# Queries, keys and maxima as float16 pairs in an encoder's attention

## The chip, the cores and the metric

The kernel runs on one core of one Trainium2 chip. The metric is the device time of one execution in microseconds (us); before the change it is 2811.22 us, the median of 3 runs (2808.62 to 2813.11). The engines are PE (TensorE: the matmuls, with PEld for its weight loads), DVE (VectorE), ACT (ScalarE), POOL (GpSimd) and SP (SyncE, which issues the DMAs here).

## The reference

Two layers on a sequence of 2048 tokens with 1024 features, all in float32. Each layer norms its input, projects it, runs a gated mixer on one half of the features and attention on the other half, projects back and adds:

```
h    = rmsnorm(x, pre_g);  proj = h @ w_in
u_a, v_a, g_a, q, k, v, g_b = split(proj)      # 512,512,512,512,128,128,512 columns
y_a  = gmlp(u_a, v_a) * silu(g_a)
q    = rope(rmsnorm(q per head, q_norm_g));  k = rope(rmsnorm(k per head, k_norm_g))
p    = softmax(q k^T / 8)                       # 8 query heads, 2 key heads, 64 wide
y_b  = (p @ v) * silu(g_b)
x    = x + rmsnorm(concat(y_a, y_b) @ w_out, post_g)
```

The inputs `q_norm_g` and `k_norm_g` are about 8, so the scores are large and the products need more than one pass of a narrow type.

## The kernel before, in words

Most large products are taken in three passes over two parts: a tensor is split into a high part of type float32r (shown as f32 in the trace; below "float32r" means this type) and a low part, and high x high, high x low and low x high are added up in PSUM.

**Projection stage of a layer** (class `Project`). Tokens go in groups of 512. `hT_jobs` norms and transposes x, `do_kv` and `do_q` norm and rotate keys and queries (`norm_rope`), and later blocks make the mixer and the gates. In `do_kv` each 128-token tile of keys `kr` is split into a rounded copy, a second copy of it and a low part (tile `kk`: two ACT copies, one POOL subtraction); four transposes per tile (two of 128 columns, two of 64) bring them under each other, and copies put them into `k_st` (the high part twice, on 128 partitions) and `k_lo` (the low part on 64 partitions, and a row of ones on partition 64, written by one DMA per layer). `do_q` writes high and low queries to the DRAM tensor `q_d`.

**Attention stage** (`attend`). A unit is 512 queries of one head; there are 32 units in a layer, each of 16 steps, one step for 128 keys. Step `k` issues on PE two matmuls into the PSUM tile `sp` (`q_st` against `k_st`: both query parts against the high keys; `q2` against `k_lo`: the high queries against the low keys, and the row of ones against the row that holds minus the maximum and a shift). ACT takes the exponential twice (`p_hi` in float16, `p_f` in float32), POOL (85% of the steps) or DVE subtracts to get the low part `p_lo` in float16, and three steps later PE multiplies `p_hi` with the values (`po`, 128x128 stationary). Once per 8 steps a **burst** of 32 matmuls, each on 32 columns of the array, adds the low parts and the sums of the denominators (`po` and `sums`). Between these stand the `max_step`s of a later unit (`pmax`: one matmul, `q_m` stationary, `k_st` moving, then a DVE reduction; 16 per unit), and `fill`, the output projection's matmuls (`pout`). When a unit's maxima are there, `max_row` reduces them, `stack_max` transposes them on PE (`t`), ACT adds the shift and writes `m_rows`, and a DMA stores them in `m_d`, from where `load_q` fetches them as the last row of `q2`. The first 8 units of a layer (`PRE`) have their maxima taken in the projection stage.

**Order.** Inside the attention loop every PE, ACT, DVE and POOL instruction keeps the order in which the code issues it (`Pinned`). In the projection stage only the matmuls and some others are pinned; a scheduler places the rest, and SP's DMAs. Jobs given to `bg.add` run a set number of ticks later. PSUM tiles share a ring of 7 banks (`ps_t`). All `Pinned` calls have line 84 in the profile.

Of the kernel before, what the change touches and what calls it, by code (L numbers as in the profile page):

```python
# [9 lines left out]
F32 = mybir.dt.float32  # L10
F32R = mybir.dt.float32r
# [27 lines left out]
def encoder(ctx: ExitStack, tc, x, w_in, w_out, pre_g, post_g, ln_a_g, ln_a_b,  # L39
# [10 lines left out]
    big = ctx.enter_context(tc.tile_pool(name="big", bufs=7))  # L50
# [8 lines left out]
    def big_t(shape, name):  # L59
        return big.tile(shape, F32R, name=name, tag="big")  # L60
# [42 lines left out]
    q_d = [dram.tile([NH, 2, HD, GRP], F32, name=f"q_d{g}") for g in range(NG)]  # L103
    m_d = [dram.tile([NH, GRP], F32, name=f"m_d{g}") for g in range(NG)]
# [70 lines left out]
    class Project:  # L175
# [11 lines left out]
        def gains(self):  # L187
# [10 lines left out]
            nc.vector.tensor_scalar_mul(self.gain_q, self.gain_q, HD ** -0.5)  # L198
# [161 lines left out]
        def do_kv(self, g, banks):  # L360
# [6 lines left out]
            for i, kr in enumerate(krs):  # L367
                for j in range(2):
                    t = g * TPG + 2 * i + j
                    kk = f_t("kk", 3 * NKV * HD).rearrange("p (k a d) -> p k a d", k=NKV, a=3)  # L370
# [4 lines left out]
                    def trans(t=t, kk=kk):  # L375
# [4 lines left out]
                        nc.scalar.copy(k_st[:, :, t * P:(t + 1) * P],  # L380
                                       pk[:, 0:2 * P].rearrange("p (k s) -> p k s", k=NKV))
                        nc.vector.tensor_copy(k_lo[0:HD, :, t * P:(t + 1) * P],
                                              pk[0:HD, 2 * P:4 * P].rearrange("p (k s) -> p k s", k=NKV))
                    bg.add(KK_DELAY + 2 * (2 * i + j), trans)

        def do_q(self, g, banks, b):
            qrs = self.norm_rope([ps.rearrange("p (t h d) -> p t h d", t=2, d=HD) for ps in banks], 4,
                                 self.rope_rows(g, self.gain_q))
            for i, qr in enumerate(qrs):
                def trans(i=i, qr=qr):  # L390
# [4 lines left out]
                    hi = f_t("fh", dt=F32R).rearrange("p (k t) -> p k t", k=2)  # L395
                    lo = f_t("fl", dt=F32R).rearrange("p (k t) -> p k t", k=2)
                    nc.scalar.copy(hi, ps)
                    nc.vector.tensor_tensor(lo, ps, hi.bitcast(F32), ALU.subtract)
                    for a, part in enumerate((hi, lo)):
                        for h in range(2):  # L400
                            dst = q_d[g][4 * b + h:4 * b + 4:2, a, :, i * 2 * P:(i + 1) * 2 * P]
                            nc.sync.dma_start(dst.rearrange("k d t -> d k t"),
                                              part.bitcast(F32)[h * HD:(h + 1) * HD])
# [212 lines left out]
    def attend(l, kv, nxt):  # L616
# [31 lines left out]
        def load_qm(u):  # L648
            qb, h = units[u]
            s = state[u]  # L650
            s.qm = f_t("q_m", dt=F32R)
            nc.sync.dma_start(s.qm.bitcast(F32), q_d[qb][h].rearrange("a d t -> (a d) t"))
            s.mx = small.tile([P, TPG, NG], F32, name="mx", bufs=3)

        def load_q(u):
            qb, h = units[u]
            s = state[u]
            s.qs = f_t("q_st", dt=F32R)
            nc.sync.dma_start(s.qs.bitcast(F32), q_d[qb][h].rearrange("a d t -> (a d) t"))
            s.q2 = f_t("q2", dt=F32R)  # L660
            nc.sync.dma_start(s.q2.bitcast(F32)[0:HD], q_d[qb][h, 0])
            nc.sync.dma_start(s.q2.bitcast(F32)[HD:HD + 1], m_d[qb][h:h + 1])
# [14 lines left out]
        def stack_max(u, pe, act):  # L677
# [4 lines left out]
            rows = small.tile([TPG, P], F32R, name="m_rows")  # L682
            act.activation(rows, ps[0:TPG, 0:P], AF.Copy, bias=EXP_SHIFT)
            nc.sync.dma_start(m_d[qb][h].rearrange("(t p) -> t p", p=P), rows.bitcast(F32))
# [528 lines left out]
```

## Time and profile before

| what | value |
|---|---|
| median of 3 runs | 2811.22 us (2808.62 to 2813.11) |
| profiled execution | 2813.78 us |
| its span, first to last instruction | 2812.0 us |
| mean granted TensorE clock | 0.993 |
| busy: PE, PEld, DVE, ACT, POOL | 97%, 74%, 67%, 56%, 46% of the span |
| DMA queue | 290.57 MB, 33.1% of 16 engines |

Layer 0 projects from 0 to about 627 us and attends until about 1410 us; layer 1 follows the same pattern to the end. In the profile a matmul's row gives its start and a modelled duration; matmuls overlap in the pipeline, so the time that a matmul takes of PE is read from start to start of rows of a steady stream, not from its own duration. A matmul that is queued early (such as the `sp` after a `po`) shows an early start; there a whole step, from one second `sp` matmul to the next, is the sound measure.

### The profile page before, as it was taken

How to read it: one execution, taken by the hardware profiler on the slowest of the kernel's cores; microseconds unless marked ns; L12 is line 12 of the kernel's file. 1: busy time of each engine (PE TensorE's matmuls, PEld its weight loads, DVE VectorE, ACT ScalarE, POOL GpSimd, SP SyncE). 2: the span in 40 equal slices, each digit the busy share in tenths (PEclk: the TensorE clock that was granted, in tenths of full speed). 3: DMA queues.
4: the chain of work that ended last, by engine and by line, in shares of the span. 5: the costliest groups of instructions: out<-in, count | busy, mean ns of one | idle time of the engine just before them, and what ended most of it. 6: DMA issues, size and time to landing. Idle time of an engine off the chain costs nothing.

```text
span 2812.0 us, 49354 instructions
## 1 busy us (share of the span) xinstructions
PE 2738.1 (97%) x18294; PEld 2067.2 (74%) x18294; DVE 1894.9 (67%) x3976; ACT 1583.3 (56%) x3295; POOL 1300.1 (46%) x1112
## 2 busy tenths in 40 slices
PE   7999999999999999999999999999999999999997
PEld 7998899885556666566699989998755666666665
DVE  7863788876666666666497639798766555656654
ACT  5322432228887777777642225322478877777774
POOL 1210121018776676666532111200377766767665
PEclk9999999999999999999999999999999999999999
DMA  4533433422222232232345343342322232221323
GB/s 134 165 110 108 137 108 90 124 90 97 85 85 89 94 91 97 87 100 89 139 151 151 122 128 121 102 124 91 112 68 94 78 100 71 83 92 59 115 71 127
DMA packets 276563, 293.71 MB, mean 104 GB/s; under 512 B 20450, under 2 KB 214306, under 8 KB 276324
## 3 DMA queue, kind: packets, MB, share of 16 engines
q1 hardware_dynamic: 276324, 290.57, 33.1%
q8 instruction: 145, 2.38, 0.3%
q14 instruction: 94, 0.77, 0.1%
HBM read 197.02 MB, written 93.45 MB: 103 GB/s over the span
## 4 chain that ended last, share of the span: by engine, by line
PE 79%; DVE 12%; ACT 4%; issue 2%; DMA 1%; POOL 1%; SPq 0%; DVEq 0%; POOLq 0%; ACTq 0%
PE pp L84 25%; PE sp L84 16%; PE pout L84 12%; PE po L84 12%; PE pmax L84 7%; PE sums L84 4%; PE pt L84 2%; DVE fc L346 2%; DVE w_lo L253 2%; ACT p_parts L84 1%; ACT p_f L84 1%; DMA w_raw<-in_w_in_dram 1%; DVE mx L670 1%; DVE o_t L84 1%; DVE fb L435 1%
## 5 line engine op out<-in xcount | busy, mean ns | idle before, releaser
L84 POOL TENSOR_TENSOR p_parts<-p_f,p_parts 128x512 f16<-128x512 f32 x872 | 1038.7, 1207 | 438.9 <-ACT p_f L84 256.7
L84 ACT ACTIVATE p_parts<-sp 128x512 f16<-128x512 f32 x1024 | 627.6, 613 | 334.5 <-PE sp L84 323.1
L84 DVE TENSOR_REDUCE mx<-pmax 128x1 f32<-128x512 f32 x768 | 515.0, 683 | 314.2 <-PE pmax L84 312.3
L84 PE MATMUL po<-p_parts,v_st 128*32 128x512 f16 (+1 forms) x3072 | 638.9, 383 | 0.0
L84 ACT ACTIVATE p_f<-sp 128x512 f32<-128x512 f32 x1024 | 629.3, 615 | 0.0
L84 PE MATMUL sp<-q_st,k_st 128*128 128x512 f32 x1024 | 578.7, 565 | 4.5 <-DVE mx L84 3.5
L84 PE MATMUL pp<-w_hi,hT 128*128 128x256 f32 x3584 | 494.8, 287 | 15.6 <-DVE hT L293 8.1
L84 PE MATMUL pout<-wo,y_t 128*128 128x512 f32 x1488 | 494.2, 397 | 0.0
L84 PEld LDWEIGHTS pp<-w_hi,hT 128*128 128x128 f32 x3584 | 461.1, 194 | 21.9 <-DVE hT L293 8.7
L84 PEld LDWEIGHTS <-v_st 128*32 128x32 f16 (+1 forms) x3072 | 193.0, 96 | 328.6 <-issue 287.4
L84 PE MATMUL pmax<-k_st,q_m 128*128 128x512 f32 x1024 | 409.7, 402 | 5.3 <-DVE mx L84 2.6
L84 PE MATMUL sp<-q,k_lo 65*128 65x512 f32 x1024 | 403.3, 394 | 0.0
L84 PEld LDWEIGHTS pout<-wo,y_t 128*128 128x128 f32 x1488 | 280.3, 189 | 60.8 <-DVE mx L84 1.7
L455 POOL TENSOR_TENSOR fl<-fa,fh 128x512 fp32r<-128x512 f32 x32 | 42.1, 1315 | 516.8 <-ACT fh L454 445.2
L84 PE MATMUL pp<-w_lo,hT 128*128 128x256 f32 x1792 | 262.4, 289 | 2.4 <-DVE w_lo L253 2.2
L84 PE MATMUL pp<-hT,w_hi 128*128 128x512 f32 x1024 | 257.8, 390 | 0.0
L84 PEld LDWEIGHTS sp<-q_st,k_st 128*128 128x128 f32 x1024 | 202.8, 198 | 65.2 <-issue 42.5
L84 PEld LDWEIGHTS pp<-w_lo,hT 128*128 128x128 f32 x1792 | 237.3, 194 | 6.6 <-DVE w_lo L253 4.8
L84 PE MATMUL sums<-p_parts,one_h 128*32 128x512 f16 x2048 | 241.8, 379 | 0.0
L252 ACT ACTIVATE w_hi<-w_raw,g_pre 128x256 fp32r<-128x256 f32 x352 | 151.8, 500 | 153.7 <-DMA w_raw<-in_w_in_dram 108.9
L84 PEld LDWEIGHTS pmax<-k_st,q_m 128*128 128x128 f32 x1024 | 193.4, 189 | 56.7 <-DVE mx L84 4.5
L84 PEld LDWEIGHTS pp<-hT,w_hi 128*128 128x128 f32 x1024 | 191.7, 188 | 39.7
(153 smaller groups left out, 3085.1 us busy)
## 6 DMA issues: line engine op xcount, KB each, us to landing
w_raw<-in_w_in_dram SPq DMA_DIRECT2D x28, 1024.0 KB
y_t<-y_d SPq DMA_DIRECT2D x56, 512.0 KB
w_raw<-in_w_in_dram SPq DMA_DIRECT2D x32, 512.0 KB
q_m<-q_d SPq DMA_DIRECT2D x64, 256.0 KB
q_st<-q_d SPq DMA_DIRECT2D x64, 256.0 KB
x_t<-in_x_dram SPq DMA_DIRECT2D x16, 512.0 KB
q_d<-fh SPq DMA_DIRECT2D x64, 128.0 KB
q_d<-fl SPq DMA_DIRECT2D x64, 128.0 KB
```

Source lines behind the costliest of these rows:

```text
L84: return tc.keep_in_program_order(call(*args, **kw))
L252: nc.scalar.activation(hi[:, d], raw[:, d], AF.Copy, scale=g)
L253: nc.vector.scalar_tensor_tensor(lo[:, d], raw[:, d], g, hi.bitcast(F32)[:, d], ALU.mult, ALU.subtract)
L346: nc.vector.tensor_tensor(t2[:, :, :, lo:lo + 16], qn[:, :, :, hi:hi + 16], tbi[:, :, 1:2, lo:lo + 16].broadcast_to([P, 2, n, 16]), ALU.mult)
L435: nc.vector.scalar_tensor_tensor(s.zt[r, c, :], pz[r, h * P:(h + 1) * P], self.lng[r, c:c + 1], self.zbias[r, c, :], ALU.mult, ALU.add)
L455: nc.gpsimd.tensor_tensor(lo, th, hi.bitcast(F32), ALU.subtract)
L670: dve.tensor_reduce(s.mx[:, j, c:c + 1], ps, AX.X, ALU.max)
```

## The change

`q_d`, `m_d`, `q_m`, `q_st`, `q2`, `k_st` and `k_lo` become float16. To keep the halves in float16's range, the key gain is divided and the query gain multiplied by a power of two taken from the key norm's weights (`gains`, eight small DVE instructions per layer more). The maximum with its shift is itself a pair of float16 (`stack_max` writes two rows: the second on DVE, and a DMA more per unit), so the second `sp` matmul has 66 rows instead of 65. Keys are no longer split ahead of the transposes: one ACT copy lays them out twice, two 128-column transposes per tile replace four, ACT rounds the result into `k_st`, and DVE subtracts it to get `k_lo`. The ones are set by a DVE memset instead of a DMA. `k_st` and `k_lo` share one buffer, and the pool of big buffers has 6 in place of 7.

```diff
-    big = ctx.enter_context(tc.tile_pool(name="big", bufs=7))
+    big = ctx.enter_context(tc.tile_pool(name="big", bufs=6))
...
-    q_d = [dram.tile([NH, 2, HD, GRP], F32, name=f"q_d{g}") for g in range(NG)]
-    m_d = [dram.tile([NH, GRP], F32, name=f"m_d{g}") for g in range(NG)]
+    q_d = [dram.tile([NH, 2, HD, GRP], F16, name=f"q_d{g}") for g in range(NG)]
+    m_d = [dram.tile([NH, 2, GRP], F16, name=f"m_d{g}") for g in range(NG)]
...
-            nc.vector.tensor_scalar_mul(self.gain_q, self.gain_q, HD ** -0.5)
+            nc.vector.tensor_reduce(top[:, 0:1], self.gain_k[:, 0], AX.X, ALU.max)
+            nc.vector.tensor_reduce(top[:, 1:2], self.gain_k[:, 0], AX.X, ALU.min, negate=True)
+            nc.vector.tensor_tensor(e, top[:, 0:1], top[:, 1:2], ALU.max)
+            ei = e.bitcast(I32)
+            nc.vector.tensor_scalar(ei, ei, EXP_BITS, None, ALU.bitwise_and)
+            nc.vector.tensor_scalar(ei, ei, float(97 << 23), float(157 << 23), ALU.max, ALU.min)
+            nc.vector.tensor_scalar(inv.bitcast(I32), ei, -1.0, float(254 << 23), ALU.mult, ALU.add)
+            nc.vector.tensor_scalar(self.gain_k, self.gain_k, inv, None, ALU.mult)
+            nc.vector.tensor_scalar(self.gain_q, self.gain_q, e, HD ** -0.5, ALU.mult, ALU.mult)
...
+                kk = f_t("kk").rearrange("p (n a d) -> p n a d", a=2, d=HD)
                 for j in range(2):
-                    nc.scalar.copy(kk[:, :, 0, :].bitcast(F32R), kr[:, j])
-                    nc.scalar.copy(kk[:, :, 1, :], kk[:, :, 0, :])
-                    nc.gpsimd.tensor_tensor(kk[:, :, 2, :], kr[:, j], kk[:, :, 0, :], ALU.subtract)
+                    nc.scalar.copy(kk[:, NKV * j:NKV * (j + 1)], kr[:, j].unsqueeze(2).broadcast_to([P, NKV, 2, HD]))
...
-                            PE.transpose(pk[:, k * P:(k + 1) * P], kk[:, k, 0:2, :], ident)
-                            PE.transpose(pk[0:HD, (2 + k) * P:(3 + k) * P], kk[:, k, 2, :], ident)
+                            PE.transpose(pk[:, k * P:(k + 1) * P], kk[:, NKV * j + k], ident)
...
+                        nc.scalar.copy(k_st[:, :, tt], pk)
+                        nc.vector.tensor_tensor(k_lo[0:HD, :, tt], pk[0:HD], k_st[0:HD, :, tt], ALU.subtract)
...
-            act.activation(rows, ps[0:TPG, 0:P], AF.Copy, bias=EXP_SHIFT)
-            nc.sync.dma_start(m_d[qb][h].rearrange("(t p) -> t p", p=P), rows.bitcast(F32))
+            for i in range(2):
+                rows = small.tile([TPG, P], F16, name="m_rows", bufs=4)
+                if i == 0:
+                    hi = rows
+                    act.activation(rows, ps[0:TPG, 0:P], AF.Copy, bias=EXP_SHIFT)
+                else:
+                    dve.scalar_tensor_tensor(rows, ps[0:TPG, 0:P], EXP_SHIFT, hi, ALU.add, ALU.subtract)
+                nc.sync.dma_start(m_d[qb][h, i].rearrange("(t p) -> t p", p=P), rows)
...
-                PE.matmul(sp, k_lo[0:HD + 1, kv, ss], s.q2[0:HD + 1], start=False, stop=True)
+                PE.matmul(sp, k_lo[0:HD + 2, kv, ss], s.q2[0:HD + 2], start=False, stop=True)
...
-        kv = [big_t([P, NKV, S], "k_st"), big_t([P, NKV, S], "k_lo")]
+        k_t = big_t([P, 2, NKV, S], "k_t", F16)
+        kv = [k_t[:, 0], k_t[:, 1]]
...
-        nc.sync.dma_start(kv[1].bitcast(F32)[HD:HD + 1].rearrange("p k (n i) -> p (k n) i", i=P),
-                          ones1.unsqueeze(1).broadcast_to([1, NKV * S // P, P]))
+        nc.vector.memset(kv[1][HD:HD + 2], 1.0)
```

On PE the end of a burst and the step behind it stand in this order before (`sums` ends the burst; `sp`, `pmax`, `po`, `pout` as above):

```order
L84 MATMUL sums<-p_parts,one_h 32x512
L84 MATMUL sp<-q_st,k_st 128x512
L84 MATMUL sp<-q_7167,k_lo 128x512
L84 MATMUL pmax<-k_st,q_m 128x512
L84 LDWEIGHTS v_st
L84 MATMUL po<-p_parts,v_st 128x512
```

The same place in the changed program (`k_t` holds `k_st` and `k_lo`):

```order
L84 MATMUL sums<-p_parts,one_h 32x512
L84 LDWEIGHTS k_t
L84 MATMUL sp<-q_st,k_t 128x512
L84 LDWEIGHTS k_t
L84 MATMUL sp<-q_7128,k_t 128x512
L84 LDWEIGHTS q_m
L84 MATMUL pmax<-k_t,q_m 128x512
L84 LDWEIGHTS v_st
L84 MATMUL po<-p_parts,v_st 128x512
```

No matmul moved; a float32r matmul brings its weight load with it in one instruction, a float16 matmul has the load as an instruction of its own ahead of it. Apart from these loads, PE's whole order differs by the 64 transposes of `kk` that are gone.

On DVE, in the start of layer 0, where `rs_*` and `x_t` norm the second to fourth token tile of x and `hT` is the low part of their transposes, before:

```order
L253 SCALAR_TENSOR_TENSOR w_lo<-w_raw,g_pre,w_hi 128x256 x5
L133 TENSOR_SCALAR rs_m<-ss_x 128x1
L134 TENSOR_SCALAR rs_x<-rs_m 128x1
L136 TENSOR_SCALAR rs_t<-rs_x,rs_m 128x1
L133 TENSOR_SCALAR rs_m<-ss_x 128x1
L137 TENSOR_SCALAR rs_x<-rs_t,rs_x 128x1
```

and in the changed program:

```order
L264 SCALAR_TENSOR_TENSOR w_lo<-w_raw,g_pre,w_hi 128x256 x5
L133 TENSOR_SCALAR rs_m<-ss_x 128x1
L201 TENSOR_REDUCE g_top<-gain_k 128x1
L134 TENSOR_SCALAR rs_x<-rs_m 128x1
L202 TENSOR_REDUCE g_top<-gain_k 128x1
L136 TENSOR_SCALAR rs_t<-rs_x,rs_m 128x1
```

The reduction of `gain_k`, which waits for that tensor's DMA, now stands in the middle of the norm of the next tiles. Behind it, where `gain_q` was scaled, stands the memset of `k_t` (2 partitions x 4096).

On DVE in the attention loop the changed program has one instruction more per unit, shown here for an early unit:

```order
L84 TENSOR_REDUCE m_neg<-mx 128x4
L84 TENSOR_REDUCE mx<-pmax 128x1 x2
L84 SCALAR_TENSOR_TENSOR m_rows<-t_7389,m_rows 4x128
L84 TENSOR_REDUCE mx<-pmax 128x1
```

`m_rows` waits there for ACT's first row; the reductions of `pmax` and DVE's share of `p_lo` stand behind it.

## Rows read from the trace of the kernel before

**Rows 1.** The page: span, busy time by engine, chain of waits by engine.

```profile
span 2812.0 us, 49354 instructions
PE 2738.1 (97%) x18294; PEld 2067.2 (74%) x18294; DVE 1894.9 (67%) x3976; ACT 1583.3 (56%) x3295; POOL 1300.1 (46%) x1112
PE 79%; DVE 12%; ACT 4%; issue 2%; DMA 1%; POOL 1%; SPq 0%; DVEq 0%; POOLq 0%; ACTq 0%
```

**Rows 2.** Waits of PE: engine line, waited for: us, times, longest.

```profile
PE t L84 <- DVE m_neg L84: 4.9, 6, 0.9
```

**Rows 3.** Stages: us, busy (instructions) by engine, PEclk, DMA share, GB/s.

```profile
600.00:840.00 240.00, 236.52 (x1529) 146.82 (x1528) 151.17 (x233) 182.50 (x363) 166.24 (x140) 1.00 0.29 93
```

**Rows 4.** Timeline of PE, first steps of layer 0's attention: start, us.

```profile
626.70 0.39 PE L84 MATMUL sp<-q_st,k_st 128*128 128x512 f32 x1
626.93 0.40 PE L84 MATMUL sp<-q,k_lo 65*128 65x512 f32 x1
...
629.27 0.39 PE L84 MATMUL pmax<-k_st,q_m 128*128 128x512 f32 x1
...
630.35 0.39 PE L84 MATMUL sp<-q,k_lo 65*128 65x512 f32 x1
...
631.04 0.40 PE L84 MATMUL sp<-q,k_lo 65*128 65x512 f32 x1
```

**Rows 5.** Timeline of PE around one burst.

```profile
802.95 0.71 PE L84 MATMUL po<-p_parts,v_st 128*128 128x512 f16 x3
803.27 0.60 PE L84 MATMUL sums<-p_parts,one_h 128*32 128x512 f16 x4
803.50 0.59 PE L84 MATMUL po<-p_parts,v_st 128*32 128x512 f16 x4
...
804.79 0.38 PE L84 MATMUL po<-p_parts,v_st 128*32 128x512 f16 x2
...
805.44 0.40 PE L84 MATMUL sp<-q,k_lo 65*128 65x512 f32 x1
```

**Rows 6.** Timeline of the weight loads around the same burst.

```profile
803.26 0.10 PEld L84 LDWEIGHTS <-v_st 128*32 128x32 f16 x2 [0.23 <-issue]
805.10 0.19 PEld L84 LDWEIGHTS sp<-q_st,k_st 128*128 128x128 f32 x1 [0.42 <-issue]
```

**Rows 7.** Groups by shape: names, shapes xcount | busy us, mean ns | idle before.

```profile
L84 PEld LDWEIGHTS <-v_st 128*128 128x128 f16 x1024 | 98.0, 96 | 273.6 <-issue 272.5 <-DVE mx L84 0.7
L84 PEld LDWEIGHTS pt<-ident,kk 128*64 128x64 f32 x64 | 7.1, 110 | 0.0
L84 ACT ACTIVATE m_rows<-t 4x128 fp32r<-4x128 f32 x48 | 12.1, 252 | 0.5 <-PE t L84 0.4
L99 DVE MEMSET one_h<- 128x32 f16 x1 | 0.1, 85 | 0.0
L473 DVE TENSOR_REDUCE v_top<-v_st 128x1 f32<-128x2048 f32 x2 | 4.5, 2270 | 0.0
```

**Rows 8.** Timeline of PE, maxima among the gate blocks of the projection stage.

```profile
559.68 0.39 PE L84 MATMUL pmax<-k_st,q_m 128*128 128x512 f32 x1
559.90 1.07 PE L84 MATMUL pp<-hT,w_hi 128*128 128x512 f32 x4
560.81 0.39 PE L84 MATMUL pmax<-k_st,q_m 128*128 128x512 f32 x1
```

**Rows 9.** Timeline of DVE at the start of layer 0.

```profile
13.23 0.21 DVE L133 TENSOR_SCALAR rs_m<-ss_x 128x1 f32<-128x1 f32 x1
15.46 0.88 DVE L283 TENSOR_SCALAR x_t<-x_t,rs_x 128x512 f32<-128x512 f32 x2
19.82 0.23 DVE L198 TENSOR_SCALAR gain_q<-gain_q 128x128 f32<-128x128 f32 x1 [1.07 <-DMA gain_q<-in_q_norm_g_dram]
23.15 0.48 DVE L253 SCALAR_TENSOR_TENSOR w_lo<-w_raw,g_pre,w_hi 128x256 fp32r<-128x256 f32 x1 [2.26 <-ACT w_hi L252]
```

**Rows 10.** Timeline of DVE at the start of layer 1.

```profile
1414.28 4.88 DVE L84 TENSOR_TENSOR hT<-pt,hT 128x512 fp32r<-128x512 f32 x8 [0.46 <-ACT hT L84]
```

More of the change, by code (lines that the diff above doesn't have):

```diff
@@ L57, in encoder, with big_t @@
     dram = ctx.enter_context(tc.tile_pool(name="dram", bufs=1, space=DRAM))
-    def big_t(shape, name):
-        return big.tile(shape, F32R, name=name, tag="big")
+    def big_t(shape, name, dt=F32R):
+        return big.tile(shape, dt, name=name, tag="big")
     def w_t(shape, name, dt=F32R):
@@ L197, in gains @@
                     nc.sync.dma_start(gv[:, :, h, :], sv[:, 1 - h, :].partition_broadcast(P))
-            nc.vector.tensor_scalar_mul(self.gain_q, self.gain_q, HD ** -0.5)
+            top = small.tile([P, 2], F32, name="g_top")
+            e = small.tile([P, 1], F32, name="g_exp")
+            inv = small.tile([P, 1], F32, name="g_inv")
+            nc.vector.tensor_reduce(top[:, 0:1], self.gain_k[:, 0], AX.X, ALU.max)
[7 more added lines that the diff above has]
+            nc.vector.tensor_scalar(self.gain_q, self.gain_q, e, HD ** -0.5, ALU.mult, ALU.mult)
         def spatial_weights(self):
@@ L367, in do_kv, with trans @@
             for i, kr in enumerate(krs):
+                kk = f_t("kk").rearrange("p (n a d) -> p n a d", a=2, d=HD)
                 for j in range(2):
[L369 to L375 removed]
+                    nc.scalar.copy(kk[:, NKV * j:NKV * (j + 1)], kr[:, j].unsqueeze(2).broadcast_to([P, NKV, 2, HD]))
+                    def trans(t=g * TPG + 2 * i + j, j=j, kk=kk):
                         pk = ps_t("pt")
                         for k in range(NKV):
[L378 to L383 removed]
+                            PE.transpose(pk[:, k * P:(k + 1) * P], kk[:, NKV * j + k], ident)
+                        pk = pk[:, 0:NKV * P].rearrange("p (k s) -> p k s", k=NKV)
+                        tt = slice(t * P, (t + 1) * P)
+                        nc.scalar.copy(k_st[:, :, tt], pk)
+                        nc.vector.tensor_tensor(k_lo[0:HD, :, tt], pk[0:HD], k_st[0:HD, :, tt], ALU.subtract)
                     bg.add(KK_DELAY + 2 * (2 * i + j), trans)
@@ L402, in trans @@
                             nc.sync.dma_start(dst.rearrange("k d t -> d k t"),
-                                              part.bitcast(F32)[h * HD:(h + 1) * HD])
+                                              part[h * HD:(h + 1) * HD])
                 bg.add(Q_DELAY + 2 * i, trans)
@@ L657, in load_q @@
             s = state[u]
[L658 to L662, printed above, removed]
+            s.qs = f_t("q_st", dt=F16)
+            nc.sync.dma_start(s.qs, q_d[qb][h].rearrange("a d t -> (a d) t"))
+            s.q2 = f_t("q2", dt=F16)
+            nc.sync.dma_start(s.q2[0:HD], q_d[qb][h, 0])
+            nc.sync.dma_start(s.q2[HD:HD + 2], m_d[qb][h])
         def max_step(u, n, pe, dve):
@@ L675, in max_row, with stack_max @@
             dve.tensor_reduce(s.m, s.mx, AX.X, ALU.max, negate=True)
-        def stack_max(u, pe, act):
+        def stack_max(u, pe, act, dve):
             s = state[u]
@@ L992, in before @@
                 bg.add(n0 + steps + 6, lambda u=u: max_row(u, nc.vector))
-                bg.add(n0 + steps + 8, lambda u=u: stack_max(u, PE, nc.scalar))
+                bg.add(n0 + steps + 8, lambda u=u: stack_max(u, PE, nc.scalar, nc.vector))
                 n0 += steps
@@ L1032, in attend @@
             at(k0 + span + 1, lambda u=u: max_row(u, DVE))
-            at(k0 + span + 3, lambda u=u: stack_max(u, PE, ACT))
+            at(k0 + span + 3, lambda u=u: stack_max(u, PE, ACT, DVE))
         def load_gb(u):
```

11 lines of the change are left out of this document (5 added, 6 removed).

## The prediction

> **What bounds the kernel now.** I read the page first, then the waits of PE, the stages, and last PE's timeline in the attention stage, because the change lies there. PE is busy for 97% of the span and makes 79% of the chain of waits [rows 1]. A busy PE need not be a full one, so the timeline decides. At the start of layer 0's attention twelve float32r matmuls of 512 columns (four rounds of the two `sp` and one `pmax`) start at 626.70 to 629.27 us: 11 intervals in 2.57 us, 0.234 us each, with no gap [rows 4]. From the second `sp` at 630.35 to the next one at 631.04 it is 0.69 us for `sp`, `sp` and one float16 `po` [rows 4]; less two of 0.234 us, `po` takes 0.222 us. In the burst the matmuls on 32 columns go four side by side: from 803.50 to 804.79 us there are six groups, 0.215 us each [rows 5]. The stage is the sum of these prices: PE has work in line nearly always, while ACT, POOL and DVE are busy 76%, 69% and 63% of the 240 us at the start of attention, its tightest part [rows 3]. What a matmul saves there comes off the time, one for one, until another engine is late.
>
> Weight loads are hidden behind the matmul before, except at the two edges of a burst. From the `po` at 802.95 to the first group of the burst at 803.27 it is 0.32 us, 0.10 more than a `po` takes [rows 5]; the float16 load at 803.26 takes 0.10 us [rows 6]. From the last group at 804.79 to the second `sp` at 805.44 it is 0.65 us: 0.215 for the group, 0.234 for the first `sp`, and 0.20 left [rows 5]; the float32r load of `sp` at 805.10 takes 0.19 us after 0.42 us of idle [rows 6]. So each edge shows one load in the open, a long one on the way out.
>
> **The matmuls.** The two `sp` (2 x 1024) and the 768 `pmax` of the attention stage change from float32r to float16: 2816 matmuls, in the same order. No row shows a float16 matmul on the full array with float16 neighbours. The bounds: 0.234 us, if the type makes no difference (saves nothing); 0.222 us, as `po` among float32r neighbours (saves 0.012 us each, 34 us); 0.215 us, a group of the burst (saves 0.019 us each, 54 us). I take 0.219 us, between the two float16 rows: 2816 x 0.015 = 42 us. `po` itself I leave at its price. The other 256 `pmax` stand in the projection stage among float32r `pp`: from one `pmax` at 559.68 to the next at 560.81 it is 1.13 us for five matmuls, 0.226 us each [rows 8]; at 0.219 us they give 256 x 0.007 = 2 us. The 66 rows in place of 65 I count as nothing: rows 4 holds matmuls of 65 and of 128 rows in one even stream of 0.23 us.
>
> By the Trainium skill, "TensorE: Matmul & The Clock Gate", section on the 56 ns gap, a warm bf16 matmul takes its columns at 2.4 GHz plus about 2.5 ns, 215.7 ns for 512. That agrees with the 0.215 us of a burst's group, and by it the sum would have 52 us in place of 42.
>
> **The edge of the burst.** The burst leaves with a load of `k_st`. Float32r takes 0.19 us there; a float16 load of 128x128 takes 96 ns [rows 7], so 0.20 us becomes about 0.10 us. There are 1024 steps / 8 = 128 bursts: 128 x 0.10 = 13 us. Bounds: 0 (the edge waits for something else than the load) to 26 us (it vanishes).
>
> **The keys.** 64 transposes of 64 columns go, each some 0.110 us of PE by its load [rows 7]: 7 us if PE is the late engine there. The projection stages have gaps about the keys, so I count half, 3.5 us (0 to 7). ACT has half the copies, POOL 32 subtractions less; neither is late. `k_lo` now waits for ACT's `k_st`, some tenths of a us behind a job that comes ticks later than the transposes: nothing.
>
> **What is added.** The memset writes 4096 elements per partition. Its bounds are 0.09 us (the memset of 32 elements) and 4.5 us (2048 elements read in 2.27 us, twice that) [rows 7]; by x_t, two of 512 elements in 0.88 us [rows 9], 3.5 us, which I take. In layer 0 it stands before 23.15 us, where DVE has 1.07 and 2.26 us of idle [rows 9]: hidden. In layer 1 it stands ahead of the eight `hT` that start at 1414.28 and take 4.88 us [rows 10], and PE needs their low halves only after the high ones: I count 2 us (0 to 3.5).
>
> The eight small instructions per layer take some 0.2 us each like `rs_m` [rows 9]. The dear one is the first, which waits for `gain_k`'s DMA behind `rs_m` at 13.23 us; behind it in line are `x_t` at 15.46 and the tiles that PE transposes next. `gain_q`, which the code loads right after `gain_k`, had landed only at 19.82 us [rows 9], so the wait lies between 0 and 6.4 us; but the next tiles then wait anyway for `w_raw` and ACT (DVE stood 2.26 us for `w_hi` at 23.15). I count 1 us for it and 1 us for layer 1. SP loses the DMA of the ones ahead of four loads of x; their users come late enough: nothing either way.
>
> `stack_max` adds 64 DVE instructions of about 0.25 us (as `m_rows` on ACT, [rows 7]) and the wait for ACT ahead of them. Behind it stand reductions of `pmax`, which hold PSUM banks, but a ring of 7 covers over three steps. PE waited for the maxima 4.9 us in six places [rows 2]; I add 1 us (0 to 10). The second `m_d` store costs SP an issue, and its reader comes many steps later.
>
> Since PE gets quicker and the rest does not, some of its gain turns into waits at the start of attention, where ACT's share rises from 76% to about 79% [rows 3]: 3 us.
>
> **Sum.** 42 + 2 + 13 + 3.5 = 60 us off, 2 + 2 + 1 + 3 = 8 us on: 52 us less. The profiled execution (2813.8 us: a span of 2812.0 and 1.8 around it) would come to 2762 us; it lies 2.6 us above the median of 2811.2, so I forecast 2760 us. Own range: 0.222 us per matmul, small edges and dear additions give about 2782; 0.215 us, the edge gone and cheap additions give about 2734.
>
> **Rivals.** *Width does not matter.* A 512-column stream may take its time by columns alone, and a load by its 128 columns. For it: `po` among float32r gains only 0.012 us. Against it: rows 6 and 7 have 0.19 us for a float32r load and 0.096 for a float16 one. Then 3.5 us off and 5 on (no gain, so no new waits): 2813 us, no change. The Trainium skill has this as a rule ("TensorE: Matmul & The Clock Gate", weight-path perf modes: one element per cell and cycle whatever its width, loads by columns and not bytes); the trace agrees with it on 32 and 128 columns of float16 and differs on the loads of the two types. If only the loads get shorter, the edge remains: 2800 us.
>
> *The loads come into the open.* A float16 matmul's load is an instruction of its own. If PE can't run it ahead of the matmul in front when that one is a full-array float16 matmul too, each `sp` and `pmax` shows 0.096 us [rows 7]: 3072 x 0.096 = 295 us, against the gains: about 3050 us, slower. It decides from some 540 exposed loads on (52 / 0.096). For it: both edges of a burst show just such a load. Against it: in the steady steps `po` has the same kind of load and costs 0.222 us, so it is hidden; within the burst they are hidden too.
>
> *ACT or POOL takes over.* With `sp` quicker, the steps without `pout` come below ACT's pace; `po` waits for exponentials and half of the gain stays behind: 2785 us. For it: ACT and POOL fall behind within a burst's eight steps. Against it: the burst itself, eight groups of 0.215 us [rows 5], gives them 1.7 us to catch up, and 76% is not full.
>
> **Chances.** Forecast 0.70; ACT or POOL 0.12; only the loads 0.06; width does not matter 0.06; loads in the open 0.06. The measurement tells 0.2% (5.6 us) from no change. Faster: 0.70 + 0.12 + 0.06 = 0.88; same 0.06; slower 0.06. The range of 2734 to 2788 us holds the forecast's and most of the third rival's.
>
> **What would show it.** In the profile after: from one second `sp` to the next, the step of `sp`, `sp`, `pmax`, `po` falls from 0.92 to about 0.88 us; the load of `sp` behind a burst takes 0.10 us and the way from the last group to the second `sp` falls from 0.65 to about 0.53; the busy shares of ACT and POOL rise by some 2% of themselves; PE still makes four fifths of the chain. If a step of three or four float16 matmuls takes 0.234 us each, the first rival holds; if it grows by 0.1 us per matmul, the second; if `po` or `sp` waits for ACT or POOL more than a few us in all, the third. Wrong altogether would be the forecast if the layer starts, not the attention stages, changed by tens of us.

## The result and the profile after

The changed kernel takes 2788.1 us (median of 4 runs, 2785.9 to 2790.5) against 2810.3 us for the kernel before on the same chip (4 runs): ratio 0.992, 95% interval 0.9903 to 0.9937. That is 22 us less, where 52 were forecast; the forecast of 2760 us is missed, and the time lies 0.1 us beyond the upper end of the range. The profiled executions are 2813.8 us before and 2785.9 after, 27.9 us apart. The first lies above all four runs of its kernel and the second is the lowest of its four, so the ledger below, which goes by these two, leaves some 6 us of the miss out.

Where the difference lies, by the starts of the same matmuls in the two traces (us):

| stage | before | after | difference | forecast |
|---|---|---|---|---|
| layer 0, first matmul to first `sp` | 615.7 | 622.2 | +6.5 | -1.8 |
| layer 0, first `sp` to last burst | 769.8 | 751.4 | -18.3 | -25.5 |
| layer 1, last burst to first `sp` | 620.1 | 626.6 | +6.5 | +0.3 |
| layer 1, first `sp` to last burst | 765.6 | 743.2 | -22.4 | -25.5 |

So the attention stages gave four fifths of what was forecast, and the projection stages, priced at next to nothing, took 13 us back.

The projection stages differ from one execution to the next. Two kernels further below, `fill_pairs` and `after_share8`, leave this stage as the changed kernel has it and take 625.5 and 623.6 us in layer 0, 629.0 and 629.2 in layer 1; `before_share8` leaves it as it was before and takes 613.2 and 616.6. By the means of these and the two of the table the projection stages lose 19 us and not 13, and then the two kernels are 22 us apart, as the medians say. The attention stages repeat far better: in three kernels that leave them alone (`memset_pool`, `gains_const`, `kk_old`) they take 751.0 to 751.5 and 743.1 to 743.2 us.

The page of the changed kernel, to be held against [rows 1]: span, busy time, chain of waits.

```profile
span 2784.1 us, 49014 instructions
PE 2681.2 (96%) x18230; PEld 1781.7 (64%) x18230; DVE 1928.6 (69%) x4056; ACT 1576.0 (57%) x3263; POOL 1279.2 (46%) x1080
PE 75%; DVE 14%; ACT 5%; issue 2%; DMA 2%; SPq 0%; POOL 0%; DVEq 0%; ACTq 0%; POOLq 0%
```

PE lost 57 us of busy time and DVE gained 34; in the chain PE falls from 79% to 75% and DVE rises from 12% to 14%.

PE's timeline of the changed kernel at the first steps of layer 0's attention, which answers to [rows 4]:

```profile
633.31 0.39 PE L84 MATMUL sp<-q_st,k_t 128*128 128x512 f16 x1
633.53 0.38 PE L84 MATMUL sp<-q,k_t 66*128 66x512 f16 x1
...
635.71 0.38 PE L84 MATMUL pmax<-k_t,q_m 128*128 128x512 f16 x1
```

Twelve matmuls start within 2.40 us: 11 intervals of 0.218 us, where float32r had 0.234. That is the forecast price (0.219). The same timeline around a burst, with the weight loads under it, for [rows 5, 6]:

```profile
805.71 0.70 PE L84 MATMUL po<-p_parts,v_st 128*128 128x512 f16 x3
806.02 0.60 PE L84 MATMUL sums<-p_parts,one_h 128*32 128x512 f16 x4
...
807.54 0.38 PE L84 MATMUL po<-p_parts,v_st 128*32 128x512 f16 x2
807.85 0.39 PE L84 MATMUL sp<-q_st,k_t 128*128 128x512 f16 x1
808.08 0.38 PE L84 MATMUL sp<-q,k_t 66*128 66x512 f16 x1
```

```profile
806.01 0.10 PEld L84 LDWEIGHTS <-v_st 128*32 128x32 f16 x2 [0.42 <-issue]
807.85 0.11 PEld L84 LDWEIGHTS <-k_t 128*128 128x128 f16 x2 [0.42 <-issue]
```

The way in is 0.31 us as before; from the last group to the second `sp` it is 0.54 us in place of 0.65. The load of `k_t` in the open takes 0.11 us in place of 0.19. Over steps of the same make-up a step with a burst lost 0.106 to 0.144 us, of which 0.018 to 0.052 went from the same step without a burst too: 0.09 to 0.095 us per edge, 128 times, 12 us where 13 were forecast.

What was not forecast shows in three places. First, a step with a `pout`:

```profile
705.72 0.38 PE L84 MATMUL sp<-q,k_t 66*128 66x512 f16 x1
705.94 0.38 PE L84 MATMUL pmax<-k_t,q_m 128*128 128x512 f16 x1
705.97 0.58 PE L84 MATMUL pout<-wo,y_t 128*128 128x512 f32 x1
706.40 0.39 PE L84 MATMUL po<-p_parts,v_st 128*128 128x512 f16 x1
706.62 0.38 PE L84 MATMUL sp<-q_st,k_t 128*128 128x512 f16 x1
706.84 0.38 PE L84 MATMUL sp<-q,k_t 66*128 66x512 f16 x1
```

1.12 us from second `sp` to second `sp`. The medians of the most common steps without a burst (us; `fp16_pout`, further below, has float16 `pout` too):

| a step of `sp`, `sp`, `po` and | places | before | changed | `fp16_pout` |
|---|---|---|---|---|
| nothing else | 26 | 0.688 | 0.653 | 0.653 |
| `pmax` | 80 | 0.920 | 0.868 | 0.868 |
| one `pout` | 74 | 0.920 | 0.897 | 0.868 |
| `pmax`, one `pout` | 258 | 1.158 | 1.117 | 1.084 |
| two `pout` | 106 | 1.158 | 1.140 | 1.084 |
| `pmax`, two `pout` | 260 | 1.391 | 1.348 | 1.299 |

In the changed kernel the first float32r matmul of a step costs 0.244 to 0.249 us and a second one behind it 0.231 to 0.243. (The start that the trace gives for it, 0.03 us behind the `pmax`, is a modelled one; the sum to the next `sp` is not.) Second, the maxima of the projection stage, the answer to [rows 8]:

```profile
566.34 0.39 PE L84 MATMUL pmax<-k_t,q_m 128*128 128x512 f16 x1
566.38 1.28 PE L84 MATMUL pp<-hT,w_hi 128*128 128x512 f32 x4
567.50 0.39 PE L84 MATMUL pmax<-k_t,q_m 128*128 128x512 f16 x1
```

Five matmuls take 1.16 us where they took 1.13 (1.158 and 1.133 in the median of 156 such places): the float16 `pmax` made its neighbourhood slower. This is not so everywhere: where eight `pp` of 256 columns stand between two `pmax` (32 places), it is 1.177 us after and 1.192 before. From the first `pmax` to the first `sp` the two layers lose 7.1 us in all. Some 3.6 of them go at the 166 places among `pp` of 512 columns; some 4.5 are waits for reductions on DVE that the kernel before hardly has; the other places give 1 back. PE's waits (us, times, longest), before and after:

```profile
PE t L84 <- DVE m_neg L675: 0.3, 2, 0.2
PE pmax L84 <- DVE mx L670: 0.2, 1, 0.2
```

```profile
PE pmax L84 <- DVE mx L677: 3.3, 5, 1.0
...
PE t L84 <- DVE m_neg L682: 1.8, 2, 0.9
```

Third, the start of layer 1, on DVE and on PE, for [rows 10]:

```profile
1403.13 3.47 DVE L1180 MEMSET k_t<- 2x4096 f16 x1 [0.91 <-issue]
1406.63 4.87 DVE L84 TENSOR_TENSOR hT<-pt,hT 128x512 fp32r<-128x512 f32 x8
```

```profile
1399.76 3.22 PE L84 MATMUL pt<-ident,x_h 128*128 128x128 f32 x28
1407.38 1.11 PE L84 MATMUL pt<-ident,x_h 128*128 128x128 f32 x4 [4.40 <-DVE hT L84]
```

The 28 transposes fill seven banks of PSUM, four in each; a bank comes free when DVE's `hT` has read it. The memset stands in front of it, and PE waits 4.40 us.

### The profile page after: what moved, and what is told of

It reads as the page before. It is cut to its first block, busy times and chain, and to the rows that moved or that the text cites. A ratio compares the mean times of both kernels' runs of the same rounds, so it can differ in the third digit from the quotient of the medians.

```text
span 2784.1 us, 49014 instructions
## 1 busy us (share of the span) xinstructions
PE 2681.2 (96%) x18230; PEld 1781.7 (64%) x18230; DVE 1928.6 (69%) x4056; ACT 1576.0 (57%) x3263; POOL 1279.2 (46%) x1080
## 4 chain that ended last, share of the span: by engine, by line
PE 75%; DVE 14%; ACT 5%; issue 2%; DMA 2%; SPq 0%; POOL 0%; DVEq 0%; ACTq 0%; POOLq 0%
PE pp L84 26%; PE sp L84 14%; PE pout L84 11%; PE po L84 11%; PE pmax L84 7%; PE sums L84 4%; PE pt L84 2%; DVE w_lo L264 2%; DVE fc L357 2%; ACT p_parts L84 2%; ACT p_f L84 2%; DVE mx L677 1%; DVE fb L442 1%; DMA w_raw<-in_w_in_dram 1%; DVE o_t L84 1%
## 5 line engine op out<-in xcount | busy, mean ns | idle before, releaser
L84 DVE TENSOR_REDUCE mx<-pmax 128x1 f32<-128x512 f32 x768 | 512.9, 681 | 210.4 <-PE pmax L84 208.5
L84 PE MATMUL pout<-wo,y_t 128*128 128x512 f32 x1488 | 656.1, 505 | 0.6 <-ACT p_f L84 0.3
L84 PE MATMUL pp<-w_hi,hT 128*128 128x256 f32 x3584 | 502.7, 289 | 14.8 <-DVE hT L304 10.1
L84 PE MATMUL pmax<-k_t,q_m 128*128 128x512 f16 x1024 | 389.3, 382 | 10.7 <-DVE mx L677 3.3
L84 PE MATMUL sp<-q_st,k_t 128*128 128x512 f16 x1024 | 389.5, 380 | 7.3 <-DVE mx L84 4.6
L84 PE MATMUL sp<-q,k_t 66*128 66x512 f16 x1024 | 390.4, 381 | 0.0
L84 PEld LDWEIGHTS <-k_t 128*128 128x128 f16 (+1 forms) x2048 | 191.4, 99 | 186.6 <-issue 73.2
L84 PE MATMUL pp<-hT,w_hi 128*128 128x512 f32 x1024 | 271.7, 413 | 0.0
L263 ACT ACTIVATE w_hi<-w_raw,g_pre 128x256 fp32r<-128x256 f32 x352 | 150.7, 499 | 171.8 <-DMA w_raw<-in_w_in_dram 111.1
L677 DVE TENSOR_REDUCE mx<-pmax 128x1 f32<-128x512 f32 x256 | 173.0, 686 | 37.0 <-PE pmax L84 35.3
```

The lines of the kernel that those rows point to most:

```text
L84: return tc.keep_in_program_order(call(*args, **kw))
L263: nc.scalar.activation(hi[:, d], raw[:, d], AF.Copy, scale=g)
L677: dve.tensor_reduce(s.mx[:, j, c:c + 1], ps, AX.X, ALU.max)
```

## The experiments

All kernels start from the changed kernel unless said otherwise. Each ratio is against runs of the kernel before on the same chip, made beside it.

**The memset.** `memset_pool`:

```
-        nc.vector.memset(kv[1][HD:HD + 2], 1.0)
+        nc.gpsimd.memset(kv[1][HD:HD + 2], 1.0)
```

> The changed kernel with one edit: the memset of the two rows of ones in k_lo goes to POOL in place of DVE. In the changed kernel's trace it takes 3.47 us on DVE, in layer 1 at 1403.13 us ahead of the hT parts (PE waited 4.40 us for them, before 0.46), in layer 0 at 19.75 us (PE's wait 4.70 became 6.70 us). Theory A: the memset is in the open in both layers; then the time falls by 5 to 8 us against the changed kernel's 2788 us, to 2780-2783, and PE's wait of 4.4 us at 1404 us is gone. Theory B: the waits come from the low-part work itself and the memset only fills them; then 2786-2790.

2781.5 us, 0.9897 (0.9882 to 0.9912): theory A. DVE's `hT` then stand at once behind ACT's copies, and PE waits as briefly as before the change (DVE, then PE, of this kernel):

```profile
1404.60 4.88 DVE L84 TENSOR_TENSOR hT<-pt,hT 128x512 fp32r<-128x512 f32 x8 [0.46 <-ACT hT L84]
```

```profile
1405.35 0.66 PE L84 MATMUL pt<-ident,x_h 128*128 128x128 f32 x4 [0.46 <-DVE hT L84]
```

From the last burst of layer 0 to the first `pmax` of layer 1 it is 451.7 us, as before the change (451.7; changed kernel 454.8). In layer 0 PE's wait for the first `hT` is shorter too; its waits for `hT` in the kernel before, the changed one and this one:

```profile
PE pp L84 <- DVE hT L293: 8.1, 3, 4.7
```

```profile
PE pp L84 <- DVE hT L304: 10.1, 3, 6.7
```

```profile
PE pp L84 <- DVE hT L304: 8.2, 3, 4.9
```

PE is some 2 us ahead by this up to 96 us; but by 140 us this kernel's PE is as late as the changed one's. So 3 us are shown in layer 1 and none that lasts in layer 0, and the rest of the 6.5 us by which the median fell is within what single runs differ by.

**The stand of DVE for ACT.** `rows_late` issues the low row of the maxima two steps later:

```
+            at(k0 + span + 5, lambda u=u: stack_low(u, DVE))
```

> The changed kernel with one edit: the low row of the maxima (scalar_tensor_tensor on DVE, and its store) is issued two steps of the program later than the high row, so that DVE does not stand for ACT's copy. In the changed kernel DVE stands 73.8 us in 48 such waits in the attention stages (1.5 us each), and PE's short waits there came to 37 us in place of 28. Theory A: DVE's stand reaches PE by late reductions of pmax and late low parts; then DVE's wait of 73.8 us goes to under 10, and 5 to 9 us of PE's waits with it: 2779-2783 us. Theory B: the buffers cover it (DVE's wait goes, PE's waits stay): 2786-2790 us.

2791.5 us, 0.9931 (0.9916 to 0.9946): theory B. The same group of DVE, in the changed kernel and in this one (busy, mean ns | idle before):

```profile
L84 DVE SCALAR_TENSOR_TENSOR m_rows<-t,m_rows 4x128 f16<-4x128 f32 x48 | 13.3, 277 | 73.8 <-ACT m_rows L84 73.8
```

```profile
L84 DVE SCALAR_TENSOR_TENSOR m_rows<-t,m_rows 4x128 f16<-4x128 f32 x48 | 13.0, 270 | 0.4 <-ACT m_rows L84 0.2
```

73 us of waiting go and the time does not fall; it lies 1.5 us above theory B's range. The attention stages take 751.4 and 744.6 us (changed kernel 751.4 and 743.2). The edit is not clean: PE now waits 3 us for `m_rows`, which it did not before, and the stages are 1.4 us longer, so the stands may have cost some 2 us and hardly more. That the ring of PSUM banks covers the most of them, as the prediction had it, agrees with this.

**Maxima in pairs.** `pmax_pairs`:

```
-                    bg.add(n0 + 4 + n, lambda u=u, n=n: max_step(...))
+                    bg.add(n0 + 4 + n // 2 * 2, lambda u=u, n=n: max_step(...))
```

> The changed kernel with one edit: in the projection stage the 256 float16 pmax are issued in pairs (each second one comes one place earlier), so that PE changes between float32r and float16 half as often. In the changed kernel a pmax and four pp of 512 columns take 1.158 us, before (all float32r) 1.133 us, though the float16 stream of the attention stage has 0.218 us per matmul and the float32r one 0.234. Theory A: a change of type costs some 20 to 30 ns there; with 128 changes to float16 and 128 back fewer, the time falls by 3 to 4 us, to 2784-2785. Theory B: a lone float16 pmax is dear for another reason (its own load, DVE's reduction): no change or, since two reductions fall together on DVE, up to 3 us more: 2788-2791.

2785.8 us, 0.9912 (0.9895 to 0.9928). The whole time can't tell 2 us, the stretch can: from first `pmax` to first `sp` it is 170.5 and 170.0 us (changed kernel 172.5 and 171.8; before 168.8 and 168.4), 3.8 us less. PE's timeline of this kernel:

```profile
560.47 0.61 PE L84 MATMUL pmax<-k_t,q_m 128*128 128x512 f16 x2
560.72 2.18 PE L84 MATMUL pp<-hT,w_lo 128*128 128x512 f32 x8
562.74 0.60 PE L84 MATMUL pmax<-k_t,q_m 128*128 128x512 f16 x2
```

Two `pmax` and eight `pp` take 2.27 us here and 2.293 in the median of 72 such places, against 2 x 1.158. So 0.02 to 0.05 us go with each second pair of type changes, among the `pp` of 512 columns: theory A.

**The gains.** `gains_const` (top, exponent and inverse left out):

```
+            nc.vector.tensor_scalar_mul(self.gain_k, self.gain_k, 0.125)
+            nc.vector.tensor_scalar_mul(self.gain_q, self.gain_q, 8.0 * HD ** -0.5)
```

> The changed kernel with the power of two of the gains replaced by constants (0.125 for the keys; 8 times the head's factor for the queries): it leaves out the calculation of that power, six small DVE instructions per layer, so a part of the computation is missing. They took 0.15 to 0.28 us each and the first did not wait for its load. Theory A: these instructions delay the chain to the first projection by their own length: about 1.5 us per layer, 2785 us. Theory B: what cost time in the projection stages is the new order of ACT's work there (w_hi ahead of the squares of q), which this edit does not touch: 2786-2789 us.

2791.7 us, 0.9929 (0.9914 to 0.9944): nothing gained. Theory A is out; B, whose range ends at 2789, is not shown by this alone.

**The keys' split.** `kk_old` puts back the key path of the kernel before (the removed lines of the diff in `do_kv`); it adds 64 transposes, and 32 copies on ACT and 32 subtractions on POOL (the text below has 64 of each).

> The changed kernel with one part of the change undone: the keys are split in front of their transposes as before (64 more transposes of 64 columns, 64 more copies on ACT, 64 more subtractions on POOL). The low parts are then those of the float32r rounding and not of the float16 one, so that the low bits of the keys are not the same. Theory A: each of the 64 transposes costs PE its 0.11 us and the four groups lose 0.2 to 0.7 us each: 7 us more than the changed kernel, 2795 us. Theory B: the order of ACT's work in the projection stages, which came with the keys' edit (w_hi ahead of the squares of q, a wait of 2 us per place), goes back too and gives 4 to 7 us: no change, 2786 to 2790.

2785.4 us, 0.9914 (0.99 to 0.9929): no change, as theory B has it. Against the kernel before, PE's starts in the changed kernel gain 0.9 us at each pair of key groups, some 7 us in all; in layer 1 they then lose 1.7 and 1.2 us at the second pair, which `kk_old` does not (0.35 and 0.2). ACT's timeline there in layer 0, changed kernel and `kk_old`:

```profile
375.29 2.51 ACT L263 ACTIVATE w_hi<-w_raw,g_pre 128x256 fp32r<-128x256 f32 x6 [2.84 <-DVE w_lo L264]
377.70 1.06 ACT L344 ACTIVATE fb<-pp 128x512 f32<-128x512 f32 x2
```

```profile
376.58 0.61 ACT L344 ACTIVATE fb<-pp 128x512 f32<-128x512 f32 x1
...
389.27 0.91 ACT L263 ACTIVATE w_hi<-w_raw,g_pre 128x256 fp32r<-128x256 f32 x2 [9.30 <-DMA w_raw<-in_w_in_dram]
```

With fewer copies in line, the scheduler puts `w_hi` ahead of the squares of q (`fb`), so these start at 377.70 us, and the chain to `fc` and its transposes is late. PE's waits (us, times, longest) for `fc`, first in the changed kernel, then in `kk_old`, where the wait for the sum (line 359) is gone:

```profile
PE pt L84 <- DVE fc L359: 6.9, 4, 2.2
...
PE pt L84 <- DVE fc L352: 2.3, 3, 0.9
```

```profile
PE pt L84 <- DVE fc L352: 3.9, 4, 2.3
```

That the keys' edit as a whole gains nothing is shown. That the order on ACT is the reason is not: `three`, further below, has the old key path and the old order too, and its PE still loses 1.3 and 1.2 us at that place of layer 1 and waits 6.5 us for `fc`.

**Fewer changes of type in attention.** `fill_pairs`:

```
+                if k % 2 == 0:
+                    pop_fill(-(-len(fill) * 2 * weight(k) // room))
```

> The changed kernel with one edit: the work of the output projection that fills the steps of the attention stage is issued at every second step, twice as much at a time, so that float32r pout stand in runs of two to four in place of one or two. Nothing else changes. Theory A (a change of type costs some 15 ns each run): with half of about 1000 runs gone 7 us go, if waits do not grow: about 2781 us. Theory B: uneven steps make the exponentials late in the steps without pout (a step of 0.65 to 0.87 us against two exponentials): PE's waits grow by more than the changes of type are worth: 2790 to 2800 us.

2792.0 us, 0.9937 (0.992 to 0.9954): theory B by the time. Layer 0's attention took 752.9 us (751.4) and layer 1's 743.2 (743.2); the third quarter of a stage got 2 to 4 us shorter and the last one 4 to 6 us longer. Theory B's reason is not borne out: PE's waits for `p_f` come to 5.6 us, as in the changed kernel. As a price of the changes it is inconclusive, since the work itself stands elsewhere.

**Float16 pairs for the output projection.** `fp16_pout` (y, its copy in DRAM and w_out):

```
-                wo[b].append(big_t([P, ND // 2, D], "wo"))
+                wo[b].append(big_t([P, ND // 2, D], "wo", F16))
-    y_d = [dram.tile([P, ND, 2, GRP], F32, name=f"y_d{g}") ...]
+    y_d = [dram.tile([P, ND, 2, GRP], F16, name=f"y_d{g}") ...]
...
```

> The changed kernel with one more group of operands as float16 pairs: those of the output projection (y, its copy in DRAM, w_out). So the float32r pout that are left among float16 matmuls in the attention stage go, and with them the changes of type. In the changed kernel a step with one pout is longer than one without by 0.244 to 0.249 us, a second pout in a row by 0.231 to 0.243, and a float16 matmul takes 0.218. Theory A: each float32r matmul has 0.231 us and each run of them 15 ns more for the change of type; then 1536 x 0.013 + 1000 x 0.015 = 35 us go if the other engines follow: 2753 us; a step of sp, sp, pmax, po, pout falls from 1.117 to about 1.087. Theory B: ACT, at 76% to 79% in that stage, is now the late one: steps get shorter where PE was late, and waits of sp, po and pmax for the exponentials take half back: 2770 us. Theory C: float16 pout is no quicker than 0.244: no change.

2759.2 us, 0.9822 (0.9808 to 0.9837): 29 us less. PE's timeline, the step to be held against that of 705.72 above:

```profile
705.57 0.38 PE L84 MATMUL sp<-q,k_t 66*128 66x512 f16 x1
...
706.01 0.38 PE L84 MATMUL pout<-wo,y_t 128*128 128x512 f16 x1
...
706.66 0.38 PE L84 MATMUL sp<-q,k_t 66*128 66x512 f16 x1
```

The medians are 0.868, 1.084 and 1.299 us with `pmax` and none, one and two `pout`: 0.2165 us for every matmul, whichever it is. Theory A's step of 1.087 us comes out at 1.084. The attention stages take 736.2 and 727.6 us, 31 less; 6 of theory A's 35 us stayed behind in stops, the time of each step beyond the median of its make-up, added up (37 us in the changed kernel, 43 here).

By the Trainium skill, "TensorE: Matmul & The Clock Gate", section on the 56 ns gap, 512 warm columns take 215.7 ns; these 0.2165 us agree. The rule that the Trainium skill has on the same page, in the section on the weight-path perf modes (one element per cell and cycle whatever its width), weighed in the prediction, does not hold for float32r here: 0.231 to 0.234 us for the same columns.

**Float16 pairs throughout.** `all_fp16` (also `hT`, `w_hi`, `w_lo` and the spatial mix, in the same manner):

> The changed kernel with all operands of the large matmuls as float16 pairs: besides those of the output projection also those of the first projections (hT, w_hi, w_lo) and of the spatial mix. In the changed kernel a float32r pp of 256 columns takes 0.120 us, one of 512 columns 0.227. Theory A: PE is the late engine in the projection stages too; float16 has 0.109 and 0.218 there, so 5376 x 0.011 + 1536 x 0.009 = 73 us go besides the 35 of the output projection: 2680 us. Theory B: PE's load was the limit of the 256-column float32r matmuls (a load of 128 x 128 in 0.19 us would not fit, so it is not), and in the projection stages DVE and ACT are the late ones: half of the 73 us turns into waits of pp for w_lo and hT: 2715 us.

2704.0 us, 0.9622 (0.9608 to 0.9637). The maxima among `pp`, PE's timeline:

```profile
539.34 0.38 PE L84 MATMUL pmax<-k_t,q_m 128*128 128x512 f16 x1
539.55 1.03 PE L84 MATMUL pp<-hT,w_hi 128*128 128x512 f16 x4
540.42 0.38 PE L84 MATMUL pmax<-k_t,q_m 128*128 128x512 f16 x1
```

1.08 us for five, 0.216 each, and from first `pmax` to first `sp` 163.9 us in both layers: less than before the change, and the loss of the changed kernel is gone. Of theory A's 73 us for the projections 55 came, so the time lies between the two theories.

**Three together.** `three` is `memset_pool`, `pmax_pairs` and `kk_old` in one.

> Three places that cost time in the projection stages are mended together, on the changed kernel: the memset on POOL, the pmax of the projection stage in pairs, the keys split in front of their transposes as before (low parts of the float32r rounding). Alone they gave 6.5, 2.3 and 2.7 us. Theory A: they are separate places (first wait of layer 1; the stretch of pmax; the stretches of the keys), so the sum holds: 2788 - 11.5 = 2776 to 2777 us, and the first pmax of layer 1 comes some 452 us behind the last burst of layer 0. Theory B: part of what each gave alone lies within the spread of single runs (about 2 us each): 2779 to 2783 us.

2778.7 us, 0.9888 (0.9871 to 0.9905), between the two: 9.4 of 11.5 us. Layer 1's first `pmax` comes 453.8 us behind the last burst, where 452 were expected.

**Memset and shares, on float16 pairs throughout.** `best_all` has the memset on POOL; `best_share8`, `best_share22` and `best_share3` also change

```
-    SHARE_0 = 15
+    SHARE_0 = 8
-    SHARE = 15
+    SHARE = 8
```

> All operands of the large matmuls as float16 pairs (2704.0 us), and the memset on POOL. Theory A: the wait of 4.4 us at the start of layer 1 is there in that kernel too, so 4 to 6 us go: 2698 to 2700 us. Theory B: with the shorter pp DVE is late at that place in any case (the waits of pp for hT grew there from 10.1 to 10.4 us): no change, 2703 to 2705.

> The same kernel with 8 in place of 15 of 100 subtractions of the low parts of the exponentials on DVE, the rest on POOL. PE's waits and short stops in the attention stages came to 28 us before the change, 37 in the changed kernel, 43 with float16 pout: they grow as PE gets quicker. Theory A: DVE is the late engine in them (waits of t for m_neg, of sp and pmax for mx, 16 us): with 70 subtractions of 0.89 us less on DVE several us go: 2692 to 2696 us. Theory B: POOL at 77% in the tightest stretch is: 70 subtractions of 1.2 us more make po wait: 2705 us or more.

> The same kernel with 22 in place of 15 of 100 subtractions on DVE. Theory A (DVE late): 3 to 8 us more than with 15, some 2705 us. Theory B (POOL late): 2 to 6 us less, some 2695 us. If neither this nor the share of 8 moves the time by over 2 us, the stops come from single places (the order of the work at the bursts and behind them) and from no engine's load.

> Float16 pairs throughout, the memset on POOL, 3 of 100 subtractions on DVE (8 gave 2695.2 us, 15 gave 2700.8). Theory A: DVE's load still tells: 2690 to 2693 us. Theory B: POOL, with 1.19 us per subtraction and 77% to 80% of the tightest stretch, is late now: 2696 to 2702 us.

2700.8 us (0.9608, 0.959 to 0.9626), 2695.2 (0.9592, 0.9576 to 0.9607), 2704.5 (0.9622, 0.9603 to 0.964) and 2695.1 (0.9604, 0.9579 to 0.963). The memset gives 3 us; less on DVE gives 5.6, more costs 3.7; 3 gives nothing beyond 8. The intervals overlap, but the attention stages of the traces bear it out: 1463.2 us with 15, 1457.6 with 8, 1468.9 with 22, 1459.4 with 3. With 3 the first four units of layer 0 take 89.0 us in place of 83.9, by one wait of PE for a reduction on DVE (PE's timeline):

```profile
629.71 0.59 PE L84 MATMUL sp<-q_st,k_t 128*128 128x512 f16 x1 [4.88 <-DVE mx L84]
```

So it is not shown that POOL is late with a share of 3. `best_share8` beats both kernels by far.

**The same share in the changed kernel and in the one before.**

> The changed kernel with 8 in place of 15 of 100 subtractions of the low parts on DVE, the rest on POOL. Theory A: the stops that were added to PE's attention stages come from DVE's load; with 62 us of DVE work less 4 to 6 us go, as with float16 pairs throughout (5.6 us): 2782 to 2784 us. Theory B: with float32r pout left, PE is slow enough for DVE; no change: 2786 to 2790 us.

> The kernel before with the same share of 8. Theory A: DVE became late only with the quicker PE: no change, 2808 to 2812 us. Theory B: DVE's load stopped PE there as much before: 4 to 6 us less, 2805 us.

2783.1 us (0.9909, 0.9894 to 0.9924) and 2804.8 us (0.9986, 0.9977 to 0.9996). By the medians both gain some 5 us, and the step between the two kernels stays 22 us; so DVE's load stopped PE before the change too. The attention stages of the traces say more: 4.0 us less before (1535.4 to 1531.4 us) and 6.9 less after (1494.6 to 1487.7).

## Why the prediction was wrong

The direction was right, and so were the two terms that carry the gain, the price of the even stream and the edge of the burst. The step that failed is what the sum made of everything outside that even stream. The 256 `pmax` of the projection stage got the even stream's price, 2 us off, and cost 7 us; a float32r `pout` among float16 matmuls has no term and cost 8 to 9; new waits were put at 3 us and came to 9; and the keys, 3.5 us off, gave nothing.

- **The matmuls (42 us).** The stream came a little better than priced: steps without `pout` lost 0.0173 us per matmul and not 0.015, by which 2816 give 49 us. But the two `sp` were taken to be alone with `po` and `pmax`. In some 700 steps a float32r `pout` stands between float16 matmuls, which before had been float32r like itself. These gained 0.009 to 0.017 us less than the same step without `pout`, some 8 us in all, 9 with the bursts'. `fp16_pout` shows the cause to be the mixed types: with one type each step is a multiple of 0.2165 us, to within 0.004.
- **The maxima of the projection stage (2 us off).** They cost 7.1 us (3.7 and 3.4): an error of 9 us and the largest term. The prediction took 0.219 us from an even stream for a matmul that stands alone among float32r. The one lone float16 matmul of the kernel before, `po`, is no warning: at 0.222 us [rows 4] it would still have had the `pmax` gain 1 us. No row of the kernel before shows the loss. Half of them go at the mixed types among `pp` of 512 columns; the other half, PE's waits for DVE's reductions, was not traced to an edit. `pmax_pairs` took half of the whole away; in `all_fp16`, where the `pp` are quicker too, it is gone.
- **The edge of the burst (13 us).** Right, 12 us.
- **The keys (3.5 us off).** PE shows 7 us less, the upper bound, but `kk_old`, without that gain, is as quick. Waits behind the keys ate it (for `fc`, `k_t` and `w_lo` 18 us in the changed kernel, 12 in `kk_old`). A new order on ACT is one likely reason, not a shown one; the prediction had looked at each engine's load there and not at the order.
- **The memset (2 us on).** 3.47 us long, as taken from `x_t`. In layer 1 it costs PE 4 us at the place and 3 us up to the maxima. The reason given, that PE needs the low halves later, overlooked that the transposes need the banks that DVE frees. In layer 0 it is not hidden either: PE's wait for `hT` grows from 4.7 to 6.7 us, though PE has lost these 2 us elsewhere by 140 us.
- **The gains (2 us on).** No wait for a DMA, and leaving six of the eight out gains nothing: about 0.
- **`stack_max` and the stand for ACT (1 us on).** 73.8 us of stands, and an effect of some 2 us at most: right.
- **New waits (3 us on).** Taking each step's time against the median of steps of its make-up, added up, stops come to 28 us before and 37 after, so 9 us; 43 in `fp16_pout`. They grow as PE gets quicker. [Rows 3], from which the 3 us come, begins 27 us ahead of the first `sp`: in the 240 us from 626 on, ACT is busy 81% and POOL 75%, not 76% and 69%, and after the change 83% and 76%. The late low row is not the cause of the extra 6 us. DVE's share is a part of it: in the attention stages a share of 8 gives 6.9 us after the change and 4.0 before, so 2 to 3 us go with DVE's load (single traces; the stops themselves fall by 3.4 and 1.3). What makes the others is not settled.

The misses add up: 9 us (maxima), 3 in the attention steps (9 at `pout` and 1 at the edge, less 7 by which the stream beat its price), 3.5 (keys), 1 to 3 (memset), 6 (stops), less 1 to 2 (gains); some 22 us, against 24 by the profiled runs (52 forecast, 27.9 come) and 30 by the medians. What is left, 2 us of the one and 8 of the other, stands in the projection stages and was not traced to an edit: in layer 0 the traces of the changed kernel and those made from it lose 2 to 4 us between 96 and 123 us, where PE waits for `fc` and `k_t`, and the rest differs from execution to execution.

The prediction's remark that the trace agrees "on 32 and 128 columns of float16" holds for the matmuls (0.215 and 0.222 us) and not for the loads: a float16 load of 32 columns takes as long as one of 128, 0.10 us [rows 6, 7].

Of the rivals, neither loads in the open nor a width that makes no difference came. "ACT or POOL takes over" had the right time, 2785 us, for the wrong reason: PE's waits for ACT's exponentials (`p_f`) came to 5.5 us, 3 more than before, and the share of 8 points to DVE, before and after.

## What to carry to other kernels

A quicker type pays by the whole stream and not by the matmul: where half of a stream is changed, count the places at which the two types meet, and don't price them with a row of an even stream. What such a place costs went by the neighbours here, so it is best measured in a small version of the mixed stream; changing the rest as well may bring more than the first half did (here 84 us after 22). Ahead of a chain at a layer's start even a 3.5 us fill belongs on an engine that has nothing to hand on. And where a scheduler orders the work, an edit that lightens one engine can move the order of what is left on it, so look at what comes first there and not only at how much there is.

## What the runs showed of the hardware

- Float16 throughout: 0.2165 us per matmul of 512 columns and 0.109 of 256; float32r 0.231 to 0.234 (0.227 among `pp`) and 0.120.
- A lone float32r matmul among float16 takes 0.244 to 0.249 us, a second one behind it 0.231 to 0.243. A lone float16 matmul among four float32r `pp` of 512 columns costs its neighbourhood so much that the five take 1.158 us, more than five float32r (1.133) or five float16 (1.08). Among eight `pp` of 256 columns it does not: the nine take 1.177 us, with a float32r one 1.192. Nor does `po` between float32r `sp`: 0.222 us.
- A float16 load of 128x128 takes 0.096 to 0.099 us, one of 128x32 0.096, a float32r load of 128x128 0.19.
- The memset of 4096 float16 elements on two partitions takes 3.47 us on DVE and 3.50 on POOL, 0.85 ns per element, as much as a float32 pass (`x_t`, 0.44 us for 512).
